# A hybrid decoder layer: attention's queries and keys ahead of its gates, scores two pairs at a time, outputs all four pairs at once, and a packed first transfer

## The chip, the core and the metric

One core of one Trainium2 chip. The metric is the device time of one execution in microseconds (us); lower is better. The engines are TensorE (PE, matrix products, with weight loads PEld beside them), VectorE (DVE), ScalarE (ACT), GpSimd (POOL) and SyncE (SP, which issues most of the transfers). SBUF is the memory the engines work from, PSUM the accumulators that PE writes to. Each engine works through its own instructions in program order.

## The reference

One layer over 256 positions of width 1,024, batch 1. Three mixers share one input projection and one output projection.

```python
def reference(x, norm_g, w_in, conv_w, conv_b, conv_ln_g, conv_ln_b, conv_pw_w, conv_pw_b, w_out, final_g):
    hn = rmsnorm(x, norm_g[0])
    proj = hn @ w_in[0]                               # 1024 -> 3840
    (a_val, a_glu, a_gate, r_q, r_k, r_v, r_gate,
     m_q, m_k, m_v, m_gate) = jnp.split(proj, SPLIT_POINTS, axis=-1)
    y_a = conformer_conv(a_val, a_glu, ...)           # GLU, causal depthwise conv of 31 taps, LayerNorm, silu, 256x256
    y_a = y_a * jax.nn.silu(a_gate)
    y_r = merge_heads(retention(...))                 # 4 heads of 64, group norm per head
    y_r = y_r * jax.nn.silu(r_gate)
    y_m = merge_heads(moba_attention(...))            # 8 heads of 64; at 256 positions: causal softmax with ALiBi
    y_m = y_m * jax.nn.silu(m_gate)
    y = jnp.concatenate([y_a, y_r, y_m], axis=-1) @ w_out[0]
    return rmsnorm(x + y, final_g)
```

The widths are 256 for the convolution, 256 for retention and 512 for attention.

## The kernel before, in words

**Products of split numbers.** Every large product is made from two parts of each float32 operand: a high part (a cast on ACT, `high`, line 115) and a low part, the remainder (a subtraction, `low`, line 121, on DVE for units in `ON_DVE`, else on POOL). A product is then three matmuls: high x high, high x low and low x high.

**Units.** Weights come as units of up to 512 KB (128 x 1,024 elements), listed in `units` in the order of their use: first ten units of the first block, then one for each name in `STEPS`, then eight of the output projection. `load` issues the transfer from SP's queue into one of seven raw buffers; `ahead(j)` (line 125) keeps loads six and casts four units ahead of unit j. A raw buffer is free again when `low` has read it, so SP waits in order for POOL or DVE.

**First block (lines 217 to 243).** Nine matmuls on constants (`p_warm`, line 75) run while the first transfers are under way. Then, for each of the eight k-chunks of 128 input channels: x's chunk (its own transfer `load_x`, 128 KB, with 16 KB of channel constants in front of the first) is scaled by the norm's weight into xh (DVE for chunk 0, ACT for the others) and xl (DVE); 1,024 weight columns are split; `first_block` runs, for each of the three products of parts, four matmuls of 256 columns for `p_a` (line 212) and two of 512 for `p_rv` (line 215), 12 and 6 in a chunk. These columns are the convolution's value and GLU halves and retention's v and gate. Then `p_rb` (line 251) spreads the row scale 1/rms.

**Steps (lines 517 to 541).** A `slot` (line 260) makes 128 output channels of a projection: 16 matmuls with the high weights (lines 266, 267), then whatever is planned `mid` for that step, then 8 with the low weights (line 272). `row` (line 277) does the same for attention's v in four quarters. After it DVE multiplies the result by the row scale (`scaled`, line 297); a gate also gets its Silu on ACT at once. Then follow the functions planned `then`, and `FILL` taps of the depthwise convolution on DVE (line 330). The order is: rq, rk (retention), ag (gate of the convolution), mv, **mg** (attention's gates), then mq0, pw, mk0, mq1, mk1, mq2, mk2, mq3, mk3 (attention's queries and keys, two heads in each: a pair).

**Attention.** For each pair, `scores` (line 434) runs its matmuls (line 439), and in the same function, for each head and each half of its rows, DVE adds the bias and takes a minimum in one instruction (line 448), ACT makes the exponential with its sum (line 450), and DVE divides (lines 455, 457) into `pr`. `turn` (line 459) transposes on PE and copies out; `values` (line 468) multiplies by v (lines 475, 477), then by the gate (line 478) and splits into yh, yl (`put_y`, lines 304, 305). These are spread over the steps: scores of pair hp in the step after mk(hp), turn two steps after that, values of pairs 0 and 1 before the scores of pairs 2 and 3, values of pairs 2 and 3 at o3. A small Exp at line 500 brings ACT's table in early.

**Output projection and end (lines 544 to 602).** `out_part` adds one k of eight to one piece of the output. k = 0 to 3 run for all pieces ("o0" to "o3", with planned work between the first two pieces and the rest), then, for each half of the rows (b), k = 4 to 7 piece by piece. For b = 1 the second half of the columns is cut into two pieces of 256. After each piece DVE adds the residual (line 581), POOL multiplies by the final norm's weight (line 583), ACT squares and sums (line 585). Then DVE forms the mean (line 588, two steps), for b = 1 adds the last piece's squares (line 592), POOL raises to -1/2 (line 593), and ACT and DVE scale (594, 598, 601) and store.

**PSUM.** Six banks (`bank`) and two more (`side`).

Of the kernel before, what the change touches and what calls it, by code (L numbers as in the profile page):

```python
# [17 lines left out]
P = 128  # L18
# [8 lines left out]
WARM = 9  # L27

RAW, PARTS = 7, 8

SPLIT_AHEAD, LOAD_AHEAD = 4, 6

ON_DVE = set(range(11))
# [8 lines left out]
    [f"mg{i}" for i in range(4)] + ["mq0", "pw"] + [f"{a}{i}" for i in range(4) for a in ("mq", "mk")][1:]  # L42
# [6 lines left out]
FILL = {"rq0": 4, "rk0": 5, "rq1": 4, "rk1": 4, "ag0": 4, "ag1": 5, "mv0": 5, "mv1": 5, "mv2": 5, "mv3": 5, "mg0": 5,  # L49
        "mg1": 5, "mg2": 6}  # L50
# [3 lines left out]
def hybrid(ctx: ExitStack, tc: tile.TileContext, xt, xn, wi, wo, taps, pw, fg, dec, bias, out):  # L54
# [19 lines left out]
    for _ in range(WARM):  # L74
        nc.tensor.matmul(p_warm, w_of(P), w_of(512), start=True, stop=True)

# [17 lines left out]
    at_step, off = {}, KC * 2 * GW  # L94
# [9 lines left out]
    raws, parts = {}, {}  # L104

    def load(j):
        src, off, n, name = units[j]
        raws[j] = rawp.tile([P, 1024], F32, name="raw_" + name, tag="raw")[:, :n]
        nc.sync.dma_start(out=raws[j], in_=src[:, off:off + n])

    def high(j):
        n, name = units[j][2:]
# [58 lines left out]
    def x_chunk(k):  # L171

        src, g = xt_sb[:, CH + k * SEQ:CH + (k + 1) * SEQ], xt_sb[:, k:k + 1]
        if k == 0:
            nc.vector.tensor_scalar(xh[:, k], src, g, None, op0=ALU.mult)
        else:
            nc.scalar.activation(xh[:, k], src, AF.Copy, scale=g)  # L177
        nc.vector.scalar_tensor_tensor(xl[:, k], src, g, xh[:, k].bitcast(F32), op0=ALU.mult, op1=ALU.subtract)  # L178
# [25 lines left out]
    def first_block(k, pieces):  # L204

        for w, part in ((0, 0), (0, 1), (1, 0)):
            for i, hi, lo in pieces:
                wt, xs = lo if w else hi, xl if part else xh
                flags = dict(start=(k == 0 and w == 0 and part == 0), stop=(k == KC - 1 and w == 1))
                if i == 0:  # L210
                    for c in range(4):
                        nc.tensor.matmul(pa[c], wt[:, c * P:(c + 1) * P], xs[:, k], **flags)  # L212
                else:
                    for b in range(2):
                        nc.tensor.matmul(pv[b], xs[:, k, b * P:(b + 1) * P], wt, **flags)  # L215

    j = 0
    load_x(0)
    for k in range(KC):
        mine = [j, j + 1] if k < 2 else [j]  # L220
        for m in mine:
            load(m)
        if k < KC - 1:
            load_x(k + 1)
# [12 lines left out]
        if k < 2:  # L237
            for i, m in enumerate(mine):
                first_block(k, [(i, *parts.pop(m))])
        else:  # L240
            hi, lo = parts.pop(j)
            first_block(k, [(i, hi[:, i * GW:(i + 1) * GW], lo[:, i * GW:(i + 1) * GW]) for i in range(2)])
        j += len(mine)
    nc.vector.tensor_copy(out=ch, in_=xt_sb[:, :CH])
# [110 lines left out]
    def conv_back():  # L355
        for c in range(2):
            p = bank(f"p_z{c}")[:, :SEQ]
# [6 lines left out]
    def conv_point():  # L364
        pwh, pwl = parts.pop(at_step["pw"])
        for c in range(2):
            p = bank(f"p_pw{c}")[:, :SEQ]
# [4 lines left out]
            put_y(c, p)  # L372
# [4 lines left out]
    def heads(p, name):  # L377

        t = work.tile([P, SEQ], F32, name=name, tag=name)
# [52 lines left out]
    mq, mk, pt, pr = {}, {}, {}, {}  # L432

    def scores(hp):
        ps = [bank(f"p_sc{hp}{a}") for a in range(2)]
# [225 lines left out]
```

## Time and profile before

| | |
|---|---|
| median of 3 runs | 138.38 us (138.36 to 138.55) |
| the profiled execution | 138.51 us |
| its span, first to last instruction | 136.7 us, 2,491 instructions |
| mean granted TensorE clock | 0.993 |
| read from HBM, written | 25.21 MB, 1.05 MB |
| PE's longest groups | p_out 3 x 14 us, p_mg, p_mq, p_mk 7.7 us per group of 32 |

The profile's views that are used: the page's table of busy time; the chain of waits, which is followed back from the last instruction to what released each step; windows, the busy time of each engine in a stretch; the timeline, with start, duration, engine, line, operation, output <- inputs, count, and in brackets the idle time before it and what ended it; and groups by line, with busy time, mean duration in ns and idle time before, by what ended it. Several instructions can be merged in one row of the timeline; the duration then runs from the first one's start to the last one's end, while in the chain it runs to the start of the next step.

### The profile page before, as it was taken

Reading aid. Unit: us, or ns where it says so; the run is one execution under the profiler, and the core shown is the slowest. Engines: PE = TensorE matmul, PEld = TensorE weight load, DVE = VectorE, ACT = ScalarE, POOL = GpSimd, SP = SyncE. Lnnn points to the kernel's source line nnn. Section 1 sums busy time; section 2 is a strip of 40 time slices with the busy share of each in tenths; the row PEclk is TensorE's granted clock in tenths of the full one; section 3 lists DMA queues with packets and bytes.
Section 4 is the critical chain, followed back from the end, with each engine's and each line's share of the span. In section 5 each row is a group of like instructions: output and inputs, shape, how many; then the busy total and the mean of one; then the engine's idle time right before and its main releaser. Section 6 shows DMA issues by size and latency. Waiting matters only on the chain.

```text
span 136.7 us, 2491 instructions
## 1 busy us (share of the span) xinstructions
PE 129.2 (94%) x909; PEld 114.9 (84%) x909; DVE 83.2 (61%) x231; ACT 72.3 (53%) x131; POOL 81.6 (60%) x51
## 2 busy tenths in 40 slices
PE   7998999999999999999999999999999999999910
PEld 2686898899998998889999999999897887778900
DVE  1546576635897789976998335857458551422360
ACT  4447689928950392016365497467448483203530
POOL 2000002696599999996769999661935839705610
PEclk9999999999999999999999999999999999999997
DMA  4999999699998798157575586655400000000114
GB/s 125 315 351 343 412 407 394 219 381 363 419 364 246 231 328 286 65 158 216 143 249 159 156 182 223 197 173 146 163 5 0 0 0 0 5 0 0 77 77 153
DMA packets 8796, 26.42 MB, mean 193 GB/s; under 512 B 1104, under 2 KB 2384, under 8 KB 8784
## 3 DMA queue, kind: packets, MB, share of 16 engines
q1 hardware_dynamic: 8496, 25.74, 55.7%
q10 hardware_dynamic: 288, 0.52, 1.0%
q8 instruction: 7, 0.11, 0.3%
q14 instruction: 5, 0.04, 0.1%
HBM read 25.21 MB, written 1.05 MB: 192 GB/s over the span
## 4 chain that ended last, share of the span: by engine, by line
PE 85%; DMA 4%; SPq 2%; issue 2%; ACT 1%; POOL 1%; DVE 1%; POOLq 0%; DVEq 0%
PE p_mv L291 8%; PE p_a L212 6%; PE p_rv L215 6%; PE p_out L197 5%; PE p_out L199 5%; PE p_out L198 5%; DMA raw_g<-in_wi 4%; PE p_mq L272 3%; PE p_mg L266 3%; PE p_mq L266 3%; PE p_mg L267 3%; PE p_mg L272 3%; PE p_mk L267 3%; PE p_mk L272 3%; PE p_mk L266 3%; PE p_mq L267 3%
## 5 line engine op out<-in xcount | busy, mean ns | idle before, releaser
L121 POOL TENSOR_TENSOR lo_o<-raw_o,hi_o 128x1024 fp32r<-128x1024 f32 x8 | 18.9, 2388 | 10.6 <-ACT hi_o L115 5.6
L330 DVE SCALAR_TENSOR_TENSOR sums<-u,tp,sums 128x256 f32<-128x256 f32 x58 | 23.7, 481 | 0.0
L197 PE MATMUL p_out<-hi_o,yh 128*128 128x512 f32 (+1 forms) x40 | 14.2, 356 | 0.0
L199 PE MATMUL p_out<-lo_o,yh 128*128 128x512 f32 (+1 forms) x40 | 14.0, 349 | 0.0
L198 PE MATMUL p_out<-hi_o,yl 128*128 128x512 f32 (+1 forms) x40 | 13.9, 349 | 0.0
L185 POOL TENSOR_TENSOR rstd<-rs_t,mhalf 128x2 f32<-128x2 f32 x1 | 0.7, 718 | 21.3 <-DVE rs_t L184 21.3
L115 ACT CAST hi_g<-raw_g 128x1024 fp32r<-128x1024 f32 (+1 forms) x10 | 8.8, 876 | 7.6 <-DMA raw_g<-in_wi 7.5
L121 POOL TENSOR_TENSOR lo_mk<-raw_mk,hi_mk 128x1024 fp32r<-128x1024 f32 x4 | 9.6, 2402 | 2.8 <-ACT hi_mk L115 2.8
L121 POOL TENSOR_TENSOR lo_mq<-raw_mq,hi_mq 128x1024 fp32r<-128x1024 f32 x4 | 9.6, 2398 | 1.7 <-ACT hi_mq L115 1.7
L121 DVE TENSOR_TENSOR lo_g<-raw_g,hi_g 128x1024 fp32r<-128x1024 f32 (+1 forms) x10 | 10.0, 1007 | 0.8 <-ACT hi_g L115 0.8
L448 DVE CUSTOM_DVE_ANT_0 p_sc<-p_sc,bias 128x256 f32<-128x256 f32 (+1 forms) x16 | 5.6, 373 | 6.8 <-ACT p_sc L450 5.0
L450 ACT ACTIVATE p_sc<-p_sc,mn 128x256 f32<-128x256 f32 (+1 forms) x16 | 6.3, 395 | 6.1 <-DVE mn L448 4.4
L121 POOL TENSOR_TENSOR lo_mg<-raw_mg,hi_mg 128x1024 fp32r<-128x1024 f32 x4 | 9.5, 2387 | 0.0
L121 POOL TENSOR_TENSOR lo_mv<-raw_mv,hi_mv 128x1024 fp32r<-128x1024 f32 x4 | 9.4, 2384 | 0.0
L197 PEld LDWEIGHTS p_out<-hi_o,yh 128*128 128x128 f32 x40 | 7.5, 188 | 1.2 <-issue 0.2
L178 DVE SCALAR_TENSOR_TENSOR xl<-xt_sb,xh 128x256 fp32r<-128x256 f32 x8 | 3.9, 485 | 7.5 <-ACT xh L177 7.4
L199 PEld LDWEIGHTS p_out<-lo_o,yh 128*128 128x128 f32 x40 | 7.5, 188 | 1.1
L198 PEld LDWEIGHTS p_out<-hi_o,yl 128*128 128x128 f32 x40 | 7.5, 188 | 1.0
L115 ACT CAST hi_o<-raw_o 128x1024 fp32r<-128x1024 f32 x8 | 8.0, 1047 | 0.0
L583 POOL TENSOR_TENSOR yg<-xn_sb,fg_sb 128x512 f32<-128x512 f32 x3 | 3.9, 1295 | 6.6 <-issue 4.1
L266 PE MATMUL p_mg<-xh,hi_mg 128*128 128x256 f32 x32 | 7.8, 282 | 0.0
L266 PE MATMUL p_mq<-xh,hi_mq 128*128 128x256 f32 x32 | 7.7, 282 | 0.0
(174 smaller groups left out, 389.9 us busy)
## 6 DMA issues: line engine op xcount, KB each, us to landing
raw_o<-in_wo SPq DMA_DIRECT2D x8, 512.0 KB, 3.8
raw_g<-in_wi SPq DMA_DIRECT2D x6, 512.0 KB, 7.7
raw_mv<-in_wi SPq DMA_DIRECT2D x4, 512.0 KB, 7.7
raw_mg<-in_wi SPq DMA_DIRECT2D x4, 512.0 KB, 4.7
raw_mq<-in_wi SPq DMA_DIRECT2D x4, 512.0 KB, 3.9
raw_mk<-in_wi SPq DMA_DIRECT2D x4, 512.0 KB, 4.3
bias<-in_bias SPq DMA_DIRECT2D x2, 768.0 KB, 8.1
raw_g<-in_wi SPq DMA_DIRECT2D x4, 256.0 KB, 3.5
```

The costliest lines, as they stand in the source:

```text
L115: nc.scalar.copy(out=hi, in_=raws[j])
L121: eng.tensor_tensor(out=lo, in0=raws.pop(j), in1=hi.bitcast(F32), op=ALU.subtract)
L197: nc.tensor.matmul(p, lh, rh, start=first, stop=False)
L198: nc.tensor.matmul(p, ll, rh, start=False, stop=False)
L199: return nc.tensor.matmul(p, lh, rl, start=False, stop=last)
L212: nc.tensor.matmul(pa[c], wt[:, c * P:(c + 1) * P], xs[:, k], **flags)
L215: nc.tensor.matmul(pv[b], xs[:, k, b * P:(b + 1) * P], wt, **flags)
L266: nc.tensor.matmul(p, hi[:, s], xh[:, k], start=(k == 0), stop=False)
L267: nc.tensor.matmul(p, hi[:, s], xl[:, k], start=False, stop=False)
L272: nc.tensor.matmul(p, lo[:, s], xh[:, k], start=False, stop=(k == KC - 1))
L291: nc.tensor.matmul(row_banks[g][b], (xl if part else xh)[:, k, b * P:(b + 1) * P], (lo if w else hi)[:, s], start=(k == 0 and w == 0 and p ...
L330: nc.vector.scalar_tensor_tensor(to[c], u[:, c, t:t + SEQ], w, sums[c], op0=ALU.mult, op1=ALU.add)
```

## The change

What it does, in four parts.

1. **Start.** x's chunks and the first block's weights lie in one array, chunk by chunk, 256 columns of x before 1,024 of weights. The first transfer (`first_sb`) holds the 32 channel constants, x's chunk 0 and its first 256 weight columns (544 columns, 272 KB). Chunk 0 then has two more transfers, chunks 1 and 2 two each (x with 512 columns, then 512), the others one of 1,280 columns. There are twelve transfers of x and weights instead of eighteen. xh is made on DVE for every chunk. The warm-up is seven matmuls of 512 columns and one of 256.
2. **Order.** The gates mg0 to mg3 come after the queries and keys. Their Silu runs for all four after mg3. The taps are filled under mq0, mk0 and mq1 instead of mg0 to mg2, and the convolution's norm, scale, back and point functions are planned one by one under mk1, mq2, mk2 and mq3.
3. **Attention.** `scores` holds only the matmuls; `exps` and `divide` hold the rest, with both halves' reductions ahead of both exponentials. Scores of pairs 0 and 1 run in the middle of mq3 (behind the pointwise product), their exps and divides after it; turn 0 after mg0; turn 1, then scores, exps and divides of pairs 2 and 3 ahead of mg2; turns 2 and 3 in o1 and o2; all values at o3, where the gate's product and the split follow for all pairs, staggered.
4. **End.** The squares are scaled inside ACT, and the two small steps of the mean come before the last piece's addition. For b = 0 the second half of the columns is scaled on DVE, after b = 1's first addition, instead of on ACT. For b = 1 the middle quarter is multiplied by the norm's weight on POOL and scaled on DVE after the last quarter.

The core of the diff:

```diff
-WARM = 9
+WARM = 7
+WIDE = SEQ + 1024
-ON_DVE = set(range(11))
+ON_DVE = set(range(13))
-    [f"mg{i}" for i in range(4)] + ["mq0", "pw"] + [f"{a}{i}" for i in range(4) for a in ("mq", "mk")][1:]
+    ["mq0", "pw"] + [f"{a}{i}" for i in range(4) for a in ("mq", "mk")][1:] + [f"mg{i}" for i in range(4)]
-... "mg0": 5, "mg1": 5, "mg2": 6}
+... "mq0": 5, "mk0": 5, "mq1": 6}
+    nc.tensor.matmul(p_warm[:, :256], w_of(P), w_of(256), start=True, stop=True)
+    CUTS = [(-SEQ, 256, 512, 1024)] + [(-SEQ, 512, 1024)] * 2 + [(-SEQ, 1024)] * (KC - 3)
     for k in range(KC):
-        for i in range(2 if k < 2 else 1):
-            n = GW if k < 2 else 2 * GW
-            units.append((wi, k * 2 * GW + i * GW, n, f"g{k}_{i}"))
+        for a, b in zip(CUTS[k], CUTS[k][1:]):
+            units.append((xw[k], SEQ + a, b - a, f"g{k}_{max(a, 0)}"))
...
-        if k == 0:
-            nc.vector.tensor_scalar(xh[:, k], src, g, None, op0=ALU.mult)
-        else:
-            nc.scalar.activation(xh[:, k], src, AF.Copy, scale=g)
+        nc.vector.tensor_scalar(xh[:, k], src, g, None, op0=ALU.mult)
...
-    load_x(0)
+    nc.sync.dma_start(out=first_sb, in_=x0)
+    raw_x[0], raws[0] = first_sb[:, CH:CH + SEQ], first_sb[:, CH + SEQ:]
...
+    def gates():
+        for hp in range(4):
+            nc.scalar.activation(mgate[:, hp], mgate[:, hp], AF.Silu)
...
+    def exps(hp):
...
             for b, s in halves:
                 nc.vector.tensor_tensor_reduce(p[:, s], p[:, s], bias_sb[...], -0.125, 3.0e38, ALU.add, ALU.min, mn[:, b:b + 1])
+            for b, s in halves:
                 nc.scalar.activation(p[:, s], p[:, s], AF.Exp, bias=mn[:, b:b + 1], scale=-1.0, accum_out=sm[:, b:b + 1])
...
+    def all_values():
+        wide = bank("p_o23")
+        po.update({0: bank("p_o0")[:, :SEQ], 1: bank("p_o1")[:, :SEQ], 2: wide[:, :SEQ], 3: wide[:, SEQ:]})
+        for hp in range(4):
+            values(hp)
+        for hp in range(4):
+            nc.vector.tensor_tensor(out=po[hp], in0=po[hp], in1=mgate[:, hp], op=ALU.mult)
+            nc.scalar.copy(out=yh[:, 4 + hp], in_=po[hp])
+            if hp:
+                low_part(hp - 1)
+        low_part(3)
...
+    plan(then, "mk1", conv_norm)
+    plan(mid, "mq2", conv_scale)
+    plan(mid, "mk2", conv_back)
+    plan(mid, "mk2", lambda: nc.scalar.activation(tiny[:, 1:2], tiny[:, 0:1], AF.Exp))
+    plan(mid, "mq3", conv_point)
+    for hp in (0, 1):
+        plan(mid, "mq3", scores, hp)
+    for f in (exps, divide):
+        for hp in (0, 1):
+            plan(then, "mq3", f, hp)
+    plan(then, "mg0", turn, 0)
+    plan(first, "mg2", turn, 1)
+    for f in (scores, exps, divide):
+        for hp in (2, 3):
+            plan(first, "mg2", f, hp)
+    plan(then, "mg3", gates)
+    plan(mid, "o1", turn, 2)
+    plan(mid, "o2", turn, 3)
+    plan(mid, "o3", all_values)
...
+            if i == 2:
+                nc.vector.tensor_tensor_reduce(sq, y[:, cs], y[:, cs], 1.0 / D, t[:, 1:2], ALU.mult, ALU.add, t[:, 2:3])
+                break
+            nc.scalar.activation(junk[:, cs], y[:, cs], AF.Square, scale=D ** -0.5, accum_out=ss2[:, b, i:i + 1])
+            nc.gpsimd.tensor_tensor(out=yg[:, cs], in0=y[:, cs], in1=fg_sb[:, cs], op=ALU.mult)
+            if i == 0 and late:
+                late.pop()()
+            if i == 1:
+                nc.vector.tensor_scalar(t[:, 0:1], ss2[:, b, 0:1], 1e-6, None, op0=ALU.add)
+                nc.vector.tensor_tensor(out=t[:, 1:2], in0=t[:, 0:1], in1=ss2[:, b, 1:2], op=ALU.add)
...
-            nc.scalar.activation(y[:, GW:], yg[:, GW:], AF.Copy, scale=r)
-            nc.sync.dma_start(out=out[rs, GW:], in_=y[:, GW:])
+            def other_half(rs=rs, y=y, yg=yg, r=r):
+                nc.vector.tensor_scalar(y[:, GW:], yg[:, GW:], r, None, op0=ALU.mult)
+                nc.sync.dma_start(out=out[rs, GW:], in_=y[:, GW:])
+            late.append(other_half)
```

More of the change, by code (lines that the diff above doesn't have):

```diff
@@ L236, in hybrid @@
             rsqrt(rstd, ss, 2, 1.0 / D, 1e-6)
[L237 to L242, printed above, removed]
+        for m, a in zip(mine, CUTS[k]):
+            first_block(k, [(max(a, 0), *parts.pop(m))])
         j += len(mine)
-    nc.vector.tensor_copy(out=ch, in_=xt_sb[:, :CH])
+    nc.vector.tensor_copy(out=ch, in_=first_sb[:, :CH])
     at["load"] = at["split"] = ROWS
@@ L371, in conv_point @@
             nc.vector.scalar_tensor_tensor(p, p, pwb[c], agate[:, c], op0=ALU.add, op1=ALU.mult)
-            put_y(c, p)
+            nc.scalar.copy(out=yh[:, c], in_=p)
+        for c, p in halves.items():
+            nc.vector.tensor_tensor(out=yl[:, c], in0=p, in1=yh[:, c].bitcast(F32), op=ALU.subtract)
     rq, rk, st = {}, {}, {}
     def heads(p, name):
-        t = work.tile([P, SEQ], F32, name=name, tag=name)
+        t = work.tile([P, SEQ], F32, name=name, tag=name[1], bufs=3)
         scaled(t, p)
@@ L461, in turn @@
             h = 2 * hp + a
-            p = bank(f"p_pt{h}")
+            p = (side if h < 4 else bank)(f"p_pt{h}")
             for o, s in ((0, 256), (P, 0), (256, P)):
                 nc.tensor.transpose(p[:, o:o + P], pr[h][:, s:s + P], ident)
-            pt[h] = work.tile([P, 384], F32, name="pt", tag="pt", bufs=4)
+            if h < 4:
+                pt[h] = work.tile([P, 384], F32, name="pt", tag="pt", bufs=4)
+            else:
+                if h == 4:
+                    pt["late"] = const.tile([P, 4, 384], F32, name="pt_late", tag="xl")
+                pt[h] = pt["late"][:, h - 4]
             (nc.scalar.copy if a else nc.vector.tensor_copy)(out=pt[h], in_=p[:, :384])
     def values(hp):
-        p = bank(f"p_o{hp}")[:, :SEQ]
+        p = po[hp]
         for part in range(2):
@@ L496, in hybrid @@
     plan(then, "mv3", ret_back)
-    plan(then, "mg3", conv_norm)
-    plan(then, "mq0", conv_scale)
-    plan(mid, "mk0", conv_back)
-    plan(mid, "mk0", lambda: nc.scalar.activation(tiny[:, 1:2], tiny[:, 0:1], AF.Exp))
-    plan(mid, "mk1", conv_point)
-    for hp in range(4):
-        k = f"mk{hp}"
-        if hp > 1:
-            plan(mid, after(k, 1), values, hp - 2)
-        plan(mid, after(k, 1), scores, hp)
-        plan(mid, after(k, 3), turn, hp)
-    plan(mid, "o3", values, 2)
-    plan(mid, "o3", values, 3)
+    plan(then, "mk1", conv_norm)
[17 more added lines that the diff above has]
+    plan(mid, "o3", all_values)
     glu(0, pa[0], pa[1])
@@ L535, in hybrid @@
                 scaled(t, p)
[L536 removed]
+                if g == "ag":
+                    nc.scalar.activation(t, t, AF.Silu)
             else:
@@ L568, in hybrid @@
             f()
+    late = []
     for b in range(2):
@@ L626 @@
     w3 = f(w_in)[0].reshape(KC, P, -1).transpose(1, 0, 2)
-    groups = [FIRST]
+    groups = []
     for name in STEPS:
```

102 lines of the change are left out of this document (49 added, 53 removed).

## The prediction

> **What bounds the kernel now.** I read the busy table and the chain of waits first.
>
> ```profile
> PE 129.2 (94%) x909; PEld 114.9 (84%) x909; DVE 83.2 (61%) x231; ACT 72.3 (53%) x131; POOL 81.6 (60%) x51
> ...
> PE 85%; DMA 4%; SPq 2%; issue 2%; ACT 1%; POOL 1%; DVE 1%; POOLq 0%; DVEq 0%
> ```
>
> TensorE (PE) is busy for 94% of the span and the chain that ends last runs on it for 85%. So a step counts if it shortens the stream of matmuls, or what lies before its first or after its last one. To see where PE is not full, I cut the span into windows.
>
> ```profile
> 10.00:15.00 5.00, 4.56 (x28) 3.73 (x27) 3.24 (x4) 2.98 (x5) 0.00 (x0) 1.00 1.02 363
> ...
> 130.40:136.70 6.30, 0.00 (x0) 0.00 (x0) 2.07 (x7) 0.72 (x1) 0.54 (x1) 0.85 0.30 113
> ```
>
> Columns are the stretch, its length, busy time of PE, weight loads, DVE, ACT, POOL, granted clock, DMA share and GB/s. PE misses 0.44 us in the third stretch of 5 us, while the DMA engines are full (1.02), and nothing after 130.40, where a tail of 6.3 us belongs to the other engines. All stretches between are full. The change can therefore win in three places: ahead of the first matmul and in the first block, in the cost of switching between kinds of matmul, and in the tail.
>
> **The head and the first block.** The timeline of PE, the chain's first long pieces, and PE's, DVE's and ACT's rows at the ends of the block:
>
> ```profile
> 0.77 4.00 PE L75 MATMUL p_warm<-const-bfloat16-1.0 128*128 128x512 bf16 x9 [0.77 <-PEq L653]
> 4.63 0.95 PE L212 MATMUL p_a<-xh,hi_g 128*128 128x256 f32 x4
> 5.42 0.28 PE L212 MATMUL p_a<-xl,hi_g 128*128 128x256 f32 x1
> ```
>
> ```profile
> 4.00 5.80 DMA raw_g<-in_wi
> 9.82 1.05 ACT hi_g L115
> 10.88 0.41 ACT xh L177
> 11.34 0.75 PE p_a L212 x4
> ```
>
> ```profile
> 28.29 0.38 PE L251 MATMUL p_rb<-ident,rstd 128*128 128x128 f32 x2
> ```
>
> ```profile
> 2.97 0.35 DVE L175 TENSOR_SCALAR xh<-xt_sb 128x256 fp32r<-128x256 f32 x1 [2.97 <-DMA xt_sb<-in_xt]
> ```
>
> ```profile
> 3.96 1.31 ACT L115 CAST hi_g<-raw_g 128x512 fp32r<-128x512 f32 x2 [1.74 <-DMA raw_g<-in_wi]
> ```
>
> The first block is eight k-chunks of equal work. From 11.34 to 28.29 PE runs the last six in 16.95 us; their first four matmuls took 0.75, where four at full speed take 0.46 (below), so an undisturbed chunk takes (16.95 - 0.29)/6 = 2.78 us, and a chunk is worth 24 matmuls of 256 columns: 0.116 us each, 0.46 for four, 0.93 for eight. Eight chunks are 22.2 us; they took 28.29 - 4.63 = 23.66, so 1.4 us are lost. About 0.33 of it is the first group, whose four matmuls lie 0.79 apart from the next group (4.63 to 5.42) where 0.46 would do: PE still runs slow. The other 1.1 is lateness: the third chunk waits for a 512 KB transfer (landed 9.82), then for the 1.05 us cast of all of it, then for ACT to make xh.
>
> What the change does to that. Warm-ups: nine run from 0.77 and the first real matmul issues at 4.63, so one takes at most 0.43. Seven and a half end by 0.77 + 7.5 x 0.43 = 4.0, 0.6 earlier. The first transfer now carries chunk 0 of x, the channel constants and the first 256 weight columns: 272 KB. Before, 144 KB had landed at 2.97 and 144 + 256 KB at 3.96; between them by size, 272 KB lands at about 3.47. Then DVE makes xh in 0.35 and ACT casts 256 columns beside it, for which 0.40 is my estimate from the 1.05 for 1,024 columns plus a start cost. So the first matmul can issue at about 3.9 to 4.0, as the warm-ups end; I take 4.0. If the larger transfer comes as late as the 400 KB did (3.96), it is 4.45.
>
> That start is early by 0.63, but the slow phase of PE ends at about 5.2 whatever runs in it (the second group, from 5.42, is at full speed). From 4.0 to 5.2 at half speed costs 0.6 instead of 0.33. The Trainium skill, "TensorE: Matmul & The Clock Gate", Part 1, speaks against counting the earlier start in full in the same way: warming is a matter of time, about 3.4 us of sustained work, not of a number of matmuls. The trace shows a longer time, about 4.4 us from 0.77 to 5.2. Without this the sum would be better by about 0.3.
>
> The 1.1 us of lateness should go. The third chunk is split (its first 512 columns come with x in one transfer, cast in half of 1.05), xh no longer stands behind the cast on ACT, and 18 issues of x and weights become 12. PE wants the third chunk at 4.0 + 0.6 + 5.56 = 10.2. Half the chunk is ahead of the 9.82 at which the whole landed; if it came no earlier, 9.82 + 0.5 = 10.3 still stalls PE only 0.1. Later chunks come with 128 x 5 KB rows instead of 1 KB and 4 KB ones, the same bytes. DVE pays for xh, 0.35 a chunk, against 2.78 of PE time in which it also makes xl and lo: hidden. So the block ends at 4.0 + 0.6 + 22.2 + 0.2 left for pieces that still come late = 27.0 against 28.29: **1.3 us** gained, between 0.7 (first matmul at 4.45, 0.3 of stalls) and 1.6.
>
> **The order of queries, keys and gates.** The same slots of the same length run in another order; PE neither gains nor loses by that. What is regrouped is the small matmuls. The chain shows what switching costs:
>
> ```profile
> 81.53 0.85 PE p_sc L439 x8
> 82.39 1.14 PE p_mq L272 x8
> ...
> 116.14 0.58 PE p_o L475 x4
> 116.72 0.22 PE p_o L477 x4
> 116.94 0.43 PE p_o L475 x4
> 117.37 0.22 PE p_o L477 x4
> 117.59 0.43 PE p_out L197
> 118.01 0.23 PE p_out L198
> ```
>
> After the scores of a pair, the eight matmuls that follow take 1.14 instead of 0.93: 0.21 to switch back. After the outputs, the first p_out takes 0.43 instead of 0.23: 0.20. The first pair of an outputs group costs 0.58 + 0.22, the next 0.43 + 0.22: 0.15 to switch in. Before there are four switches back after scores, one after outputs, and three entries into outputs (pairs 0 and 1 alone, 2 and 3 together). Afterwards scores come in two groups and outputs in one: two returns and two entries fewer, 2 x 0.21 + 2 x 0.15 = **0.7 us**.
>
> What can eat this is the softmax. All of two pairs' DVE work, eight score halves, now stands at the end of slot mq3, ahead of the scaling of mk3 and mg0 and of the copies in the transposes, and turn(0) on PE follows two slots (2 x 2.78 = 5.6 us) later.
>
> ```profile
> L457 DVE TENSOR_SCALAR pr<-p_sc,ri 128x256 f32<-128x256 f32 (+1 forms) x16 | 5.9, 413 | 0.3
> L448 DVE CUSTOM_DVE_ANT_0 p_sc<-p_sc,bias 128x256 f32<-128x256 f32 (+1 forms) x16 | 5.6, 373 | 6.8 <-ACT p_sc L450 5.0 <-PE p_sc L439 1.7
> ...
> L448 DVE DVE_READ_ACCUMULATOR2_ANT mn<- 128x1 f32 x16 | 2.3, 142 | 0.0
> ```
>
> After the scaling of mq3 (about 0.5 us) DVE does eight L448 (3.0 us) and then pair 0's four L457 and two reciprocals (4 x 0.41 + about 0.3 = 2.0): 5.5 us by these means, and less where neighbours overlap. The 5.0 us that L448 waited for ACT came from a second half standing behind the first half's Exp; in the new order both reductions come before both Exps, so that wait goes: pair 0's Exps run on ACT while DVE reduces pair 1. So turn(0) finds its input just in time; if the eight read-outs of accumulators lie beside nothing, PE stands for 8 x 0.14 = 1.1 less the 0.1 of slack. I take 0, by the overlaps. Banks: two pairs hold four of six score banks, mg1 is the first slot to need one back, after turn(0), and pair 0's first division frees it before turn(0) can start. The extra switch of ACT to Silu for the gates lies behind all Exps, and the gates are first used after the last outputs: hidden; without that cover a table load and four gates, some 3 us, would show. The weight casts behind the Exps on ACT are for slots at least three steps (8 us) off.
>
> The outputs of all pairs at o3 are followed on PE by 1.4 us of k=3 work (six 512-column equivalents) before the first y is read; pair 0's product, cast and remainder start when its own outputs are done, some 2 us earlier. Hidden.
>
> **The tail.** DVE, POOL and ACT rows of the end:
>
> ```profile
> 130.42 0.42 DVE L581 TENSOR_TENSOR xn_sb<-p_out,xn_sb 128x256 f32<-128x256 f32 x1 [0.97 <-PE p_out L199]
> 130.76 0.14 DVE L588 TENSOR_SCALAR fin_t<-ss 128x1 f32<-128x1 f32 x1
> 131.01 0.21 DVE L588 TENSOR_SCALAR fin_t<-ss,fin_t 128x1 f32<-128x1 f32 x1
> 131.26 0.48 DVE L592 CUSTOM_DVE_ANT_0 sq<-xn_sb,fin_t 128x256 f32<-128x256 f32 x1
> ```
>
> ```profile
> 128.45 1.30 POOL L583 TENSOR_TENSOR yg<-xn_sb,fg_sb 128x512 f32<-128x512 f32 x1 [1.07 <-DVE xn_sb L581]
> 131.83 0.54 POOL L593 TENSOR_TENSOR fin_r<-fin_t,mhalf 128x1 f32<-128x1 f32 x1 [2.08 <-DVE fin_t L592]
> ```
>
> ```profile
> 128.59 0.73 ACT L601 ACTIVATE xn_sb<-yg,fin_r 128x512 f32<-128x512 f32 x1 [0.45 <-ACT xn_sb L594]
> ...
> 129.84 0.40 ACT L585 ACTIVATE junk<-xn_sb 128x256 bf16<-128x256 f32 x1
> ```
>
> Between the last addition and the last sum of squares stand two tiny fin_t steps, 130.76 to 131.26: 0.5 us. They now come before that addition. They need the square that ACT started at 129.84; without the 0.73 of L601, which moves to DVE, ACT can start it as soon as its addition is there, about 0.4 earlier, and be done by 130.1, so fin_t ends by about 130.4, when PE delivers the last piece. Gain **0.45 us**; if fin_t holds up the addition instead, 0.2 lost. The two last output pieces start as before, the second behind the first's issue: 0.
>
> POOL now multiplies the middle quarter as well, about 0.65 (half of 1.30), after the 1.30 at 128.45: done by 130.4, a microsecond ahead of the power at 131.4. It has a neighbour on DVE, the other half of rows 0 to 127. What such a neighbour can cost:
>
> ```profile
> 25.28 3.16 POOL L121 TENSOR_TENSOR lo_rk<-raw_rk,hi_rk 128x1024 fp32r<-128x1024 f32 x1 [1.82 <-ACT hi_rk L115]
> 28.40 2.39 POOL L121 TENSOR_TENSOR lo_rq<-raw_rq,hi_rq 128x1024 fp32r<-128x1024 f32 x1
> ```
>
> The same subtraction took POOL 0.77 longer when DVE subtracted beside it. That puts the multiplication's end at 131.2, still ahead. The Trainium skill, "GPSIMD Engine Reference", 1 Specifications, gives the reason to expect it: both share SBUF interfaces, with contention when DVE has two SBUF inputs or a two-port mode. The sum is the same by row and by rule, with 0.2 left over.
>
> **Sum.** 1.3 + 0.7 + 0.45 = 2.45 us off the profiled execution's 138.51: 136.06. The median of the runs before, 138.38, lies 0.13 below that execution, so I say 135.9.
>
> **Rivals.** (B) *Arrival bounds the first block.* For: DMA share 1.02 while PE waits, equal bytes. Against: the third chunk's half and its shorter cast. Gain at the head 0.7, result 136.5. (C) *DVE delays turn(0)*, by up to 1.0: 136.9. For: the means leave 0.1; against: the overlaps. (D) *The fast clock comes later.* If a gap between the last warm-up and the first real matmul restarts its 4.4 us, full speed comes at 8.4 instead of 5.2: 3.2 us at half speed lose 1.6, 137.5. For: the larger first transfer may be late. Against: the new count of warm-ups ends where I expect the first transfer's cast to end. The Trainium skill, same page and part, says that the window (3.4 us) runs freely, which makes the moment of the flip vary. (E) *Slower.* The softmax of two pairs still alternates between DVE and ACT. With its waits a half cost DVE (5.6 + 6.8)/16 = 0.78 before; eight are 6.2, with 0.5 and 2.0 turn(0) starts 8.7 us after mq3 instead of 5.6, PE stands for 3.1, and the result is 139.0. It decides from a stall of 2.45, that is, pair 0's division ending later than 8.1 us after mq3. For: that row of waits. Against: both reductions come first now, and the four tiles are separate. (F) *The change doesn't do what it says:* the transfers and groups land on cover that exists, the time stays at 138.4.
>
> **Chances.** Forecast, 135.3 to 136.4: 0.60. B 0.12, C 0.12, D 0.05, E 0.07, F 0.04. The range 135.2 to 137.2 takes in the forecast, B and C. Faster by over 0.2% (0.28 us, about what a measurement of this kernel can tell from no change): 0.89; same 0.04; slower 0.07.
>
> **What would show it.** Right: first p_a at about 4.0; no idle PE before p_rb, which issues at about 27.0; one group of 16 p_o L475 with a single 0.58; L448 without waits for ACT; the last addition followed at once by L592's square. Wrong: idle PE before p_pt or at p_a of chunk three or five, a first group still at half speed after 5.5, or fin_t waiting for ACT ahead of the last addition.

## The result, and the profile after

The changed kernel takes 136.77 us (median of 6 runs, 136.6 to 137.32), the kernel before 138.37 (6 runs, 138.27 to 138.71): ratio 0.9885, 95% interval 0.9865 to 0.9906. It is faster by 1.6 us; 2.45 were forecast, and the predicted 135.9 is 0.9 too low, inside the range of 135.2 to 137.2 but outside the forecast's own 135.3 to 136.4. The profiled execution took 137.11 us (span 135.3), 1.40 less than the one of before. One later repeat's (a2's) profiled execution took 185.17 us at a granted clock of 0.66, and one execution of e9 took 447.92 us; neither is read here.

The page's busy table, the chain's shares and the windows of the changed kernel (same columns as in the prediction):

```profile
PE 128.2 (95%) x908; PEld 115.6 (85%) x908; DVE 86.6 (64%) x241; ACT 70.3 (52%) x126; POOL 81.6 (60%) x52
...
PE 87%; DMA 4%; POOL 2%; issue 1%; SPq 1%; DVE 1%; ACT 0%; POOLq 0%; DVEq 0%
```

```profile
8.00:10.00 2.00, 1.59 (x13) 1.33 (x12) 1.96 (x5) 1.61 (x3) 0.00 (x0) 1.00 1.04 424
10.00:15.00 5.00, 5.00 (x32) 4.46 (x32) 4.01 (x8) 1.93 (x3) 0.00 (x0) 1.00 1.01 386
```

PE still carries the chain. The stretch from 10 to 15, where PE missed 0.44 before, is full now; PE misses 0.41 between 8 and 10 instead. So the wait did not go: it moved from the third k-chunk to the second. The chain of waits shows that and the whole path (start, time to the next step, step):

```profile
2.10 5.88 DMA raw_g<-in_xw
8.00 0.63 ACT hi_g L121
8.67 1.68 PE p_a L211 x12
...
28.58 0.44 PE p_rb L247 x4
...
83.10 1.51 PE p_sc L442 x16
84.61 1.14 PE p_mq L268 x8
...
95.46 1.51 PE p_sc L442 x16
96.97 0.32 PE p_mg L262
...
113.87 0.58 PE p_o L489 x4
114.45 0.22 PE p_o L491 x4
114.67 0.43 PE p_o L489 x4
...
116.62 0.43 PE p_out L196
...
126.65 0.70 DVE xn_sb L617
...
131.12 0.48 DVE xn_sb L635
```

Two steps cut the span into three parts that can be compared with any other kernel of this case: the chain's `p_rb`, which ends the first block, and the addition of the first piece of rows 128 to 255 (`xn_sb`, 0.70 us), where the last tail begins. The last row, `xn_sb` with 0.48 us, is a scaling, the last work of the chain. In the chain of before they stand here:

```profile
28.45 0.44 PE p_rb L251 x4
...
127.62 0.70 DVE xn_sb L581
...
132.41 0.48 DVE xn_sb L598
```

So the start took 28.45 before and 28.58 now (0.13 longer; 1.3 less was forecast), the middle 99.17 and 98.07 (1.10 less; 0.7 was forecast), the tail, up to the span's end, 9.08 and 8.65 (0.43 less; 0.45 was forecast). Up to the last scaling, 0.32 of that is won (4.79 before, 4.47 after). One execution of the start is not a measurement of it, as the experiments show.

The head of the changed kernel in the timeline, PE first, then ACT:

```profile
3.97 0.77 PE L211 MATMUL p_a<-xh,hi_g 128*128 128x256 f32 x2
...
5.84 0.63 PE L211 MATMUL p_a<-xl,hi_g 128*128 128x256 f32 x2
6.27 0.60 PE L211 MATMUL p_a<-xh,lo_g 128*128 128x256 f32 x2
6.70 0.63 PE L214 MATMUL p_rv<-hi_g,xh 128*128 128x512 f32 x2
7.17 0.63 PE L214 MATMUL p_rv<-hi_g,xl 128*128 128x512 f32 x2
```

```profile
3.46 0.41 ACT L121 CAST hi_g<-first_sb 128x256 fp32r<-128x256 f32 x1 [1.24 <-DMA first_sb<-in_x]
...
5.51 0.62 ACT L121 CAST hi_g<-raw_g 128x512 fp32r<-128x512 f32 x1 [1.29 <-DMA raw_g<-in_xw]
8.00 1.28 ACT L121 CAST hi_g<-raw_g 128x512 fp32r<-128x512 f32 x2 [1.87 <-DMA raw_g<-in_xw]
```

The first transfer landed at 3.46 (3.47 was estimated), its cast took 0.41 (0.40) and the first matmul issued at 3.97 (4.0). But two matmuls of 256 columns stand 0.43 apart up to 6.70, and two of 512 then 0.47: PE ran at about half speed until 6.7, while the granted clock in the windows stands at 1.00 throughout. And chunk 1's first transfer was cast at 8.00, so PE had the next work at 8.67.

The tail: POOL, DVE and POOL again in the timeline of the changed kernel:

```profile
127.49 2.09 POOL L624 TENSOR_TENSOR yg<-xn_sb,fg_sb 128x512 f32<-128x512 f32 x2 [0.94 <-DVE xn_sb L617]
```

```profile
129.05 0.54 DVE L630 TENSOR_TENSOR fin_t<-fin_t,ss 128x1 f32<-128x1 f32 x1 [0.38 <-ACT junk L623]
129.52 0.41 DVE L617 TENSOR_TENSOR xn_sb<-p_out,xn_sb 128x256 f32<-128x256 f32 x1
129.97 0.49 DVE L620 CUSTOM_DVE_ANT_0 sq<-xn_sb,fin_t 128x256 f32<-128x256 f32 x1
```

```profile
130.54 0.54 POOL L631 TENSOR_TENSOR fin_r<-fin_t,mhalf 128x1 f32<-128x1 f32 x1 [0.96 <-DVE fin_t L620]
```

The last addition is followed at once by its square, as forecast, and POOL's extra multiplication has been over for 0.96 us when its power starts.

### The profile page after: what moved, and what is told of

Read it like the earlier page. It is cut to its first block, busy times and chain, and to the rows that moved or that the text cites. A ratio compares the mean times of both kernels' runs of the same rounds, so it can differ in the third digit from the quotient of the medians.

```text
span 135.3 us, 2484 instructions
## 1 busy us (share of the span) xinstructions
PE 128.2 (95%) x908; PEld 115.6 (85%) x908; DVE 86.6 (64%) x241; ACT 70.3 (52%) x126; POOL 81.6 (60%) x52
## 4 chain that ended last, share of the span: by engine, by line
PE 87%; DMA 4%; POOL 2%; issue 1%; SPq 1%; DVE 1%; ACT 0%; POOLq 0%; DVEq 0%
PE p_mv L287 8%; PE p_a L211 7%; PE p_rv L214 7%; PE p_out L196 5%; PE p_out L198 5%; PE p_out L197 5%; DMA raw_g<-in_xw 4%; PE p_mg L262 3%; PE p_mq L268 3%; PE p_mk L263 3%; PE p_mq L263 3%; PE p_mq L262 3%; PE p_mk L268 3%; PE p_mk L262 3%; PE p_mg L268 3%; PE p_mg L263 3%
## 5 line engine op out<-in xcount | busy, mean ns | idle before, releaser
L121 ACT CAST hi_g<-raw_g 128x512 fp32r<-128x512 f32 (+2 forms) x11 | 8.8, 797 | 8.1 <-DMA raw_g<-in_xw 8.0
L127 DVE TENSOR_TENSOR lo_g<-raw_g,hi_g 128x512 fp32r<-128x512 f32 (+2 forms) x11 | 9.8, 905 | 1.8 <-ACT hi_g L121 1.7
L624 POOL TENSOR_TENSOR yg<-xn_sb,fg_sb 128x512 f32<-128x512 f32 (+1 forms) x4 | 4.7, 1177 | 9.1 <-issue 6.7
L263 PE MATMUL p_mk<-xl,hi_mk 128*128 128x256 f32 x32 | 7.7, 279 | 0.0
L263 PE MATMUL p_mq<-xl,hi_mq 128*128 128x256 f32 x32 | 7.7, 279 | 0.0
```

What stands on the lines that cost most here:

```text
L121: nc.scalar.copy(out=hi, in_=raws[j])
L127: eng.tensor_tensor(out=lo, in0=raws.pop(j), in1=hi.bitcast(F32), op=ALU.subtract)
L263: nc.tensor.matmul(p, hi[:, s], xl[:, k], start=False, stop=False)
```

## The experiments

All kernels are edits of the changed one. "p_rb" and "addition" are the two steps of the chain, "middle" runs from the first to the second, "tail" from the addition to the span's end, which is given to 0.1 us. "Full speed" is the issue of the first matmul that stands 0.12 from the next (at 256 columns; before, 0.21), good to about 0.1 us. Three groups of kernels ran beside the kernel before, whose medians were 138.71 (e1 to e4), 138.40 (a2, e2b, e6, e7) and 138.84 (e9, e1b, e5, e10); across groups the ratios are compared.

| kernel | median us | ratio, 95% | full speed | p_rb | addition | middle | tail |
|---|---|---|---|---|---|---|---|
| before | 138.37 | 1 | 5.2 | 28.45 | 127.62 | 99.17 | 9.08 |
| after | 136.77 | 0.9885 (0.9865, 0.9906) | 6.7 | 28.58 | 126.65 | 98.07 | 8.65 |
| a2_after_again | 136.70 | 0.9862 (0.9837, 0.9888) | | | | | |
| e1_old_head | 137.19 | 0.9898 (0.9876, 0.9920) | 6.7 | 28.32 | 126.41 | 98.09 | 8.79 |
| e1b_old_head_again | 137.49 | 0.9899 (0.9868, 0.9931) | 6.4 | 28.98 | 127.19 | 98.21 | 8.81 |
| e9_middle_only | 137.91 | 0.9934 (0.9907, 0.9961) | by 5.4 | 28.90 | 127.11 | 98.21 | 9.09 |
| e2_old_tail | 136.84 | 0.9867 (0.9843, 0.9891) | 6.0 | 27.97 | 126.05 | 98.08 | 9.05 |
| e2b_old_tail_again | 136.73 | 0.9875 (0.9852, 0.9898) | 4.8 | 27.85 | 125.93 | 98.08 | 8.97 |
| e3_scores_apart | 137.33 | 0.9909 (0.9883, 0.9935) | 5.9 | 27.86 | 126.78 | 98.92 | 8.62 |
| e7_values_apart | 137.03 | 0.9892 (0.9871, 0.9913) | 5.9 | 27.93 | 126.74 | 98.81 | 8.66 |
| e4_paced | 137.37 | 0.9914 (0.9889, 0.9938) | 6.0 | 28.23 | 127.18 | 98.95 | 8.72 |
| e6_contig | 136.56 | 0.9868 (0.9841, 0.9895) | 6.3 | 27.70 | 125.78 | 98.08 | 8.62 |
| e5_warm9 | 136.58 | 0.9840 (0.9808, 0.9872) | by 4.7 | 28.22 | 126.30 | 98.08 | 8.70 |
| e10_contig_fin | 136.73 | 0.9853 (0.9819, 0.9886) | 5.5 | 28.17 | 126.25 | 98.08 | 8.55 |

**The old start (e1), and the changed kernel again (a2).** e1 takes x's own transfers, the nine warm-ups, the eighteen issues and ACT's xh from the kernel before, and leaves the rest changed.

```diff
-WARM = 7
+WARM = 9
-    CUTS = [(-SEQ, 256, 512, 1024)] + [(-SEQ, 512, 1024)] * 2 + [(-SEQ, 1024)] * (KC - 3)
-        for a, b in zip(CUTS[k], CUTS[k][1:]):
-            units.append((xw[k], SEQ + a, b - a, f"g{k}_{max(a, 0)}"))
+        for i in range(2 if k < 2 else 1):
+            n = GW if k < 2 else 2 * GW
+            units.append((wi, k * 2 * GW + i * GW, n, f"g{k}_{i}"))
...
-    nc.sync.dma_start(out=first_sb, in_=x0)
+    load_x(0)
```

> The changed kernel with the old start: own transfers for x, old pieces of the first block, nine warm-ups, xh on ACT. My theory: the new start gave nothing, because the second chunk lands 1.4 us later than it did and PE runs slow for 1.6 us longer; the attention part and the tail gave 1.1 and 0.45 us. Then this is 138.4 - 1.55 = 136.8, the same as the changed kernel within 0.3, with p_rb at about 28.3 us. Rival: the new start gains half a microsecond or more in most executions and the profiled one was unlucky; then this is 137.3 or more.

> The changed kernel itself, beside the others of this call. The moment at which PE comes to full speed (matmuls of 256 columns 0.12 apart instead of 0.21) was 6.6 us in its first profile and 5.7 to 5.8 in two kernels with the same start. My theory now: that moment is drawn anew in each execution, and with the new start p_rb follows it, about half a microsecond for each microsecond; so this profile shows p_rb between 27.8 and 28.6, and times spread over about 0.7 us around 136.8. Rival: the moment is fixed by the program; then it is 6.6 again and p_rb at 28.6.

e1 ran at 0.9898, the changed kernel again at 0.9862. With the first 0.9885 the mean of the changed kernel is 0.9874, 0.0025 or 0.34 us below e1; the intervals overlap. On the scale of 138.4 e1 makes 137.0, between its theory (136.8) and its rival (137.3). In e1's profile PE waited for nothing in the first block, although the third chunk came as late as before, where its cast began at 9.82:

```profile
9.71 1.05 ACT L116 CAST hi_g<-raw_g 128x1024 fp32r<-128x1024 f32 x1 [1.78 <-DMA raw_g<-in_wi]
```

PE was at half speed until 6.7 there and came to the second chunk 0.7 later than before (8.44 against 7.75), so the same lateness was hidden: the third chunk began at 11.24, against 11.34. So a wait of 0.44 us in one execution is no measure of what its removal gives; it depends on how late PE itself is. a2's own profile cannot decide between its theory and its rival, but e2 and e2b below can: they are one program and came to full speed at 6.0 and at 4.8, so the program does not fix that moment.

**The old tail (e2, and e2b again).** The body of the loop over pieces is that of before: two fin_t steps behind the last addition, ACT scales rows 0 to 127, POOL multiplies no middle quarter.

```diff
-                nc.vector.tensor_scalar(t[:, 0:1], ss2[:, b, 0:1], 1e-6, None, op0=ALU.add)
-                nc.vector.tensor_tensor(out=t[:, 1:2], in0=t[:, 0:1], in1=ss2[:, b, 1:2], op=ALU.add)
+        for i in range(2):
+            nc.vector.tensor_scalar(t[:, i:i + 1], ss2[:, b, i:i + 1], 1.0 / D, t[:, 0:1] if i else 1e-6, op0=ALU.mult, op1=ALU.add)
...
-            late.append(other_half)
+            nc.scalar.activation(y[:, GW:], yg[:, GW:], AF.Copy, scale=r)
+            nc.sync.dma_start(out=out[rs, GW:], in_=y[:, GW:])
```

> The changed kernel with the old end (other half of rows 0 to 127 on ACT, fin_t after the last addition, two products with the norm's weight at the very end). Theory: the new end is worth 0.4 to 0.45 us, so 137.2. Rival: its gain is eaten by fin_t, which now holds up the last addition; then 136.8, no change against the changed kernel.

> The changed kernel with the old end, once more, beside the changed kernel. By the stages of its first profile the old end takes 0.4 us longer from the addition of rows 128 to 255 onward, but its median was no later than the changed kernel's. Theory: the stage holds and the start scattered: 0.3 to 0.5 slower than the changed kernel here. Rival: the new end wins nothing: equal.

The tail grew to 9.05 and 8.97, 0.3 to 0.4 more, as expected; the medians did not (0.9867 and 0.9875, the changed kernel 0.9885 and 0.9862). By time alone these two runs do not show the end's gain.

**Middle only (e9), and the old start again (e1b).** e9 has the old start and the old tail; e1b differs from it by the tail alone.

> Both ends as before (the old loading and warm-up, the old layer norm of the last rows); only the attention's order, its grouping and the place of the conversions are the changed kernel's. Theory: the middle alone is worth 1.1 us, so this runs 1.1 under the kernel before (137.3 if that shows 138.4), with a stage from the first key product's result to the last rows' addition of 98.1 instead of 99.2. Rival: the gain in the middle hangs on the new start; then the stage stays at 98.6 or more and the time is 137.8 or more.

> The old start with the new middle and the new end, beside e9 which differs from it by the end alone; the old start varies less, so the end's worth should show. Theory: the new end saves 0.35 to 0.45 against e9 (the last stage 8.7 to 8.8 instead of 9.05). Rival: the end's gain is taken back by what follows it, and the two agree within 0.1.

e9 gains 0.0066 or 0.9 us (interval 0.5 to 1.3) by the middle alone; its middle part takes 98.21 instead of 99.17. e1b stands another 0.42 lower (137.91 to 137.49), and its tail is 8.81 instead of 9.09. Here the end's gain can be seen in the time too, if only just: the executions overlap (137.34 to 138.23 and 136.76 to 137.77). The chain at e1b's start:

```profile
2.57 5.12 DMA raw_g<-in_wi
7.75 0.50 issue
8.25 0.51 ACT xh L178
8.80 1.86 PE p_a L213 x12
```

In e1b and e9 the old start had its wait too, but at the second chunk, not at the third as in the trace of before. With e1, the old start gave 28.45, 28.32, 28.98 and 28.90 for p_rb, a mean of 28.66; the new one, in the five profiles with that start as it is (after, e2, e2b, e3, e7), 28.58, 27.97, 27.85, 27.86 and 27.93, a mean of 28.04. That is 0.6 us for the new start, half of what was forecast.

The four combinations of start and tail give the same by time, as means of the ratios:

| | old tail | new tail |
|---|---|---|
| old start | 0.9934 | 0.9898 |
| new start | 0.9871 | 0.9874 |

The new start is worth 0.0044, 0.6 us, on average over both tails (0.9 and 0.3), the tail 0.0016, 0.2 us (0.5 and 0), the middle 0.9 us. Each ratio has an interval of some 0.0025 on either side, so the differences between 0.9 and 0.3 and between 0.5 and 0 are not told apart, nor is the tail's 0.2 from nothing. What the tail is worth is read from the stages of the profiles.

**Scores in four groups (e3).** Each pair's scores run alone, in mq3, mk3 and twice at mg2.

```diff
-    for hp in (0, 1):
-        plan(mid, "mq3", scores, hp)
+    for hp, k in ((0, "mq3"), (1, "mk3")):
+        plan(mid, k, scores, hp)
+        plan(then, k, exps, hp)
+        plan(then, k, divide, hp)
```

> The changed kernel with each pair's scores, exponentials and divisions on their own: pair 0 in mq3, pair 1 in mk3, pair 2 ahead of mg2, pair 3 in the middle of mg2; order and everything else as changed. Theory: grouping gives the gain of the middle: two more returns at 0.21 and two second pairs at 0.85 instead of 0.66, so 0.8 slower, 137.6. Rival: the new order gives it by itself; then 136.8.

```profile
82.44 0.85 PE p_sc L442 x8
83.29 1.13 PE p_mq L268 x8
...
86.29 0.85 PE p_sc L442 x8
87.14 1.14 PE p_mk L268 x8
```

The middle took 98.92, 0.85 more than the changed kernel's 98.07. The chain says why: two pairs apart cost 2 x 0.85 and two returns; together they cost 1.51 and one. So a group that is saved is worth 0.21 for the return and 0.19 (2 x 0.85 - 1.51) for the entry. The prediction had only the first.

**Outputs in three groups (e7).** Pair 0's outputs run behind mg3, pair 1's behind o0, pairs 2 and 3 at o3.

```diff
-        for hp in range(4):
-            values(hp)
+        values(2)
+        values(3)
...
+    plan(then, "mg3", one_value, 0)
+    plan(then, "o0", one_value, 1)
```

> The changed kernel with the outputs of pairs 0 and 1 moved out of the common group, pair 0 after mg3 and pair 1 after o0, their gate and split still at o3. Theory: two more entries at 0.15 and two more returns at 0.20: 0.7 slower from p_rb to the addition of rows 128 to 255. Rival: entries and returns lie in the shadow of weight loads and cost nothing by themselves: no change.

```profile
102.12 0.58 PE p_o L489 x4
102.71 0.22 PE p_o L491 x4
102.93 0.43 PE p_out L196
103.35 0.23 PE p_out L197
```

The middle took 98.81, 0.74 more: two entries of 0.15 (0.58 against 0.43) and two returns of 0.20 (0.43 against 0.23) make 0.70.

**Pieces held back (e4).** Theory: the transfers that were issued at once share the DMA engines and so all come late. Three raw buffers are held and freed one by one as DVE gets through chunk 0.

```diff
+    hold = [rawp.tile([P, WIDE], F32, name=f"hold{i}", tag="raw") for i in range(3)]
...
+        if k == 0:
+            let_go()
```

> The changed kernel with three raw buffers held back at first: chunk 2's two transfers and chunk 3's are issued when the first three low parts are made (about 4.7, 5.1 and 6 us) instead of at 3.0 to 4.1. Theory: transfers in flight share the DMA engines, and what was issued behind chunk 1 delayed it; with less behind it chunk 1 lands at about 6.5 to 7 instead of 8.0, the gap of 0.6 us ahead of it on PE goes, and the time is 136.2. Rival: chunk 1 is late for another reason (its rows, its place in memory); it still lands at 8.0, and the later chunks come later too: 136.8 to 137.5.

```profile
6.25 0.62 ACT L121 CAST hi_g<-raw_g 128x512 fp32r<-128x512 f32 x1 [2.02 <-DMA raw_g<-in_xw]
7.55 1.27 ACT L121 CAST hi_g<-raw_g 128x512 fp32r<-128x512 f32 x2 [0.68 <-DMA raw_g<-in_xw]
```

The held transfers were issued until 6.1 us instead of 4.7. Chunk 0's last piece came at 6.25, not earlier than the 5.51 of the changed kernel, and chunk 1's at 7.55, inside the 7.1 to 8.0 seen without the hold. So nothing of what the theory expected (6.5 to 7) shows in this one profile. This kernel's middle also took 98.95, each slot 2.88 instead of 2.80; why is open.

**Each piece stored in one stretch (e6).** The other theory for the late landing: the rows of a piece lie 5 KB apart in HBM. Here each piece is a block of its own.

```diff
+            n, at_x = b - a, P * (k * WIDE + SEQ + a)
+            src = bass.AP(tensor=xw.tensor, offset=xw.offset + at_x, ap=[[n, P], [1, n]])
+            units.append((src, 0, n, f"g{k}_{max(a, 0)}"))
```

> The changed kernel with each transfer of x and weights of the first block stored in one run of memory, instead of columns cut out of rows of 5 KB; same sizes, same order. Theory: cutting 2 KB and 3 KB out of 5 KB rows is what made chunk 0's third transfer land 0.9 us and chunk 1's first 0.6 to 1.5 us later than the same bytes before; now the third lands at about 4.6 and chunk 1 at about 6.5, no gap on PE, and p_rb comes at about 27.5 (0.3 to 0.6 faster than the changed kernel). Rival: the order and the sizes of the transfers make them late, wherever the rows lie: no change.

```profile
6.88 1.29 ACT L127 CAST hi_g<-raw_g 128x512 fp32r<-128x512 f32 x2 [0.80 <-DMA raw_g<-in_xw]
```

```profile
7.44 0.63 PE L220 MATMUL p_rv<-lo_g,xh 128*128 128x512 f32 x2
7.91 0.64 PE L217 MATMUL p_a<-xh,hi_g 128*128 128x256 f32 x4
```

Chunk 1 landed at 6.88, PE waited for nothing, and p_rb at 27.70 is the earliest of all. But the time (136.56) lies inside the changed kernel's interval, and e10, which stores the pieces in the same way, had chunk 1 at 7.61 and p_rb at 28.17. Not settled. The rows show something else: with no wait at all chunk 1's first matmul still issued at 7.91, because PE ran at half speed until 6.3: 4.0, plus 2.8 for a chunk, plus half of the 2.3 us at half speed, is 7.95.

**The old number of warm-ups (e5).** Nine instead of seven and a half, all else as changed.

```diff
-WARM = 7
+WARM = 9
...
-    nc.tensor.matmul(p_warm[:, :256], w_of(P), w_of(256), start=True, stop=True)
```

> The changed kernel with the old length of the warm-up: nine products of full width and no half one, so that the first matmul on real data comes at about 4.6 instead of 4.0. Theory: what comes before full speed and before the landing of chunk 1 has slack, so the later start costs 0 to 0.3 (136.7 to 137.0). Rival, as the prediction had it: each 0.1 us of the start is worth as much at the end; then it costs 0.6 (137.3).

```profile
4.21 0.78 PE L210 MATMUL p_a<-xh,hi_g 128*128 128x256 f32 x2
...
6.92 0.73 PE L213 MATMUL p_rv<-hi_g,xh 128*128 128x512 f32 x2 [0.77 <-ACT hi_g L120]
```

The time is 136.58, the lowest ratio of all (0.9840), though not apart from the changed kernel's. The rival's 137.3, a ratio of 0.992, lies outside its interval. In the profiled execution full speed came by 4.7, so the nine warm-ups cost 0.24 (4.21 against 3.97) and not 0.6, and PE went through chunk 0's first half sooner and stood for 0.77 until its third transfer. Nothing was lost by the later start; what is early is only early for the next wait.

**One operand as a scalar (e10).** As e6, and the last fin_t step in another form.

```diff
-                nc.vector.tensor_tensor(out=t[:, 1:2], in0=t[:, 0:1], in1=ss2[:, b, 1:2], op=ALU.add)
+                nc.vector.tensor_scalar(t[:, 1:2], ss2[:, b, 1:2], t[:, 0:1], None, op0=ALU.add)
```

> The changed kernel with each chunk of rows stored in one piece per partition (as in e6) and the last sum of two statistics written with one of them as a scalar operand. Theory: that small addition takes about 0.2 instead of 0.54 us beside GpSimd's multiplication, which delayed the last addition by about 0.07, so the time is that of e6 or 0.1 less: 136.45 to 136.6. Rival: the small addition takes 0.5 in this form too, and the time is that of e6.

```profile
128.65 0.22 DVE L636 TENSOR_SCALAR fin_t<-ss,fin_t 128x1 f32<-128x1 f32 x1 [0.52 <-ACT junk L629]
129.05 0.42 DVE L623 TENSOR_TENSOR xn_sb<-p_out,xn_sb 128x256 f32<-128x256 f32 x1 [0.18 <-PE p_out L204]
```

The step takes 0.22 instead of 0.54, the addition waits for PE again, and from the first addition to the last scaling it takes 4.41 instead of 4.47, the shortest. The time, 136.73, shows nothing of it. No version here beats the changed kernel by more than its interval.

## Why the prediction was right and where it failed

**Right: the way the kernel is bound.** PE carried the chain before and after, and all three places where the prediction looked for a gain gave one, the tail by the profiles' stages alone. That the time came out inside the range is in part luck: the middle gave 0.4 more than forecast, the start 0.7 less.

**The middle: the mechanism was right, the size too small.** 0.7 was forecast as two returns after scores (2 x 0.21) and two entries into outputs (2 x 0.15). The profile has 1.10, and e9 alone 0.9 in time. The missing term is the entry into scores: a second pair in the same group costs 0.66 (1.51 - 0.85), not 0.85, so two entries of 0.19 go as well: 0.42 + 0.30 + 0.38 = 1.10. The trace of before could not show it, since every pair stood alone there. It did show the same for outputs, 0.58 for a first pair and 0.43 for the next; the prediction used that row for the outputs and left it out for the scores.

**Rivals C and E did not happen.** PE waits for nothing after the first block. DVE's reductions hardly wait any more:

```profile
L452 DVE CUSTOM_DVE_ANT_0 p_sc<-p_sc,bias 128x256 f32<-128x256 f32 (+1 forms) x16 | 5.5, 378 | 0.9 <-PE p_sc L442 0.6
```

0.9 us of idle time in front of sixteen, where it was 6.8 before, and none of the named releasers is an Exp. The assumption that both reductions ahead of both exponentials end the alternation was right.

**The tail: 0.45 forecast, 0.32 by its edit.** From the first addition to the last scaling the chain takes 4.79 in the four profiles with the old tail and 4.46 or 4.47 in the eight with the new one (e10 left out). The rest of the 0.43 lies behind the last scaling: up to the span's end it is 4.31 on average in the four profiles with the old start and 4.19 in the nine with the new one, whichever the tail. So some 0.1 goes with the start's edit; why is open. That 0.43 lies so near to 0.45 is luck. Two things were mis-sized. Taking out the two fin_t steps was booked as 0.5, but the first of them began 0.34 after the last addition's start and the square cannot follow before 0.45: 0.84 (131.26 - 130.42) became 0.45 (129.97 - 129.52), 0.39. And, the case that the prediction named last, fin_t waits 0.38 for ACT's square and then takes 0.54 instead of 0.21, which pushes the addition by 0.07 (from the first addition to the last 2.87 in the changed kernel, 2.80 in e10).

The 0.54 comes with the step's new form, not with POOL's extra multiplication: for rows 0 to 127, where POOL multiplied in both kernels, the same step took 0.21 in the old form (the kernel before) and 0.60 in the new one:

```profile
126.30 0.21 DVE L588 TENSOR_SCALAR fin_t<-ss,fin_t 128x1 f32<-128x1 f32 x1 [0.73 <-ACT junk L585]
```

```profile
125.33 0.60 DVE L630 TENSOR_TENSOR fin_t<-fin_t,ss 128x1 f32<-128x1 f32 x1 [0.73 <-ACT junk L623]
```

The Trainium skill, "GPSIMD Engine Reference", 1 Specifications, names the condition, DVE instructions with two SBUF inputs; here the form with two such inputs took 0.54 beside POOL's multiplication, and the form with one of them as a scalar pointer 0.22. No run has the two-input form without POOL beside it, so POOL's share in the 0.54 is not shown.

**The start: 1.3 forecast, 0.6 on average, less than nothing in this execution.** Two steps failed.

*"The slow phase of PE ends at about 5.2 whatever runs in it."* It ends at a moment that differs from execution to execution: between 4.7 (or a little earlier) and 6.7 in thirteen profiles, all with their first matmul between 0.77 and 0.78, and at 6.0 and 4.8 in e2 and e2b, which are one program. The Trainium skill, "TensorE: Matmul & The Clock Gate", Part 1, says of this that the window runs freely and the moment varies with the phase, and gives a width of about 3.4 us. The runs agree that it varies: 3.9 to 5.9 us after the first matmul. The prediction quoted that rule for rival D and yet took one execution's 5.2 as a constant. In the changed kernel it was 6.7: (6.7 - 4.0)/2 = 1.35 us instead of the 0.6 in the sum. No gap on PE had restarted anything, as D had supposed, and D's 8.4 was not seen. But the old start has the same draw, so this does not explain the mean; and alone it does not explain the scatter either, as a2's theory had it (half a microsecond at p_rb for each one here): e2b reached full speed 1.2 earlier than e2 and p_rb 0.12 earlier, and e6, with 6.3, has the earliest p_rb of all.

*"The 1.1 us of lateness should go."* This is the step that was worth most and failed. Its causes as the prediction named them, the transfer, the cast and ACT's xh of the third chunk, did go: in all nine profiles with x and weights packed, nothing is late after the second chunk, and every chunk from the third on takes about 2.80. From the second chunk's first matmul to p_rb the chain takes 19.8 or 19.9 in all nine (28.58 - 8.67 in the changed kernel, 27.70 - 7.91 in e6), and 20.7, 19.9, 20.2 and 20.1 with the old start (before, e1, e1b, e9). That is 0.3 on average, in place of the 1.1. The second chunk itself begins at 8.16 on average in the five profiles with the new start as it is, and at 8.45 in the four with the old one, another 0.3; the sum had it at 4.0 + 0.6 + 2.8 = 7.4 and did not ask when its weights land.

So the new start is worth what the second chunk's start is worth: 6.8 if nothing were slow or late, 7.4 as forecast, 7.9 to 8.7 as measured. Three things hold it there, and the latest counts: PE's slow phase (7.91 in e6, with no wait), the landing of chunk 0's third transfer (cast at 5.88 in e3 and at 6.25 in e4 and e5, where PE waits for it and for nothing after), and the landing of chunk 1, which was cast from 6.9 to 8.0 with the new start. In the changed kernel's own profile it was the last one: its cast at 8.00 would have held PE until 8.67 however early full speed had come. With the old start the same number of bytes (1,040 KB) was cast at this:

```profile
7.72 0.62 ACT L116 CAST hi_g<-raw_g 128x512 fp32r<-128x512 f32 x1 [1.95 <-DMA raw_g<-in_wi]
```

in e9, and at 6.39 in e1. Landing varies by a microsecond in both, so no sign is left that packing brought it forward, and neither holding pieces back (e4) nor storing them apart (e6 and e10) did so beyond the scatter. What sets it is open. An earlier first matmul is worth nothing against it: e5 started 0.24 later at no cost.

**Rival B happened in part.** It gave the head 0.7 and the time 136.5, for "arrival bounds the first block". Arrival and the slow phase together leave it 0.6, though at the second chunk and at chunk 0's last piece, and not at the third half-transfer that B had in mind. By the profiles the parts are 0.6, 1.1 and 0.4 (with the 0.1 behind the last scaling), 2.1 together; the ratios of the changed kernel's two measurements make 1.6 (1.3 to 1.9) and 1.9 (1.5 to 2.3). The parts come out above the first of these intervals. They rest on one profile of the kernel before and few of the others, and where the difference lies is open.

## What to carry to other kernels

A chain of waits at the start of a kernel is one draw: before a wait is booked as a gain, look at a second execution, and ask who would be late next if it went, here the chunk before. Switching between kinds of matmul costs on both sides, on entry and on return, so count both for each group that is saved; two edits of the order here gave back what that count said, to 0.05 us. And when a small step is moved, keep its form, or time the new one: an addition of 128 numbers written with two tensors in place of a scalar operand took 0.3 us longer here.

## What was not expected of the hardware

- PE runs at about half speed for 3.9 to 5.9 us after the first matmul, differing between two executions of one program by 1.2 us (e2 and e2b), with the granted clock in the profile's rows at 1.00 all the time (windows from 0.77 to 8 us of both kernels).
- An addition of 128 x 1 numbers on DVE took 0.54 to 0.60 us with two SBUF tensors as inputs while POOL multiplied, and 0.21 to 0.22 with one of them as a scalar pointer, POOL multiplying too.
- The first 1,040 KB of x and weights, brought by four or five transfers, landed between 6.4 and 8.0 us in different executions. The DMA share stood between 0.8 and 1.2 in the windows from 2 to 8 us of the kernel before and the changed one.
